# Four units of a recurrent projection begun early, their partial sums parked in SBUF

## The chip, the cores and the metric

One core of a Trainium2 chip. The metric is the device time of one execution in microseconds (us). Engines: PE is TensorE (matmul), PEld its weight loads, DVE VectorE, ACT ScalarE, POOL GpSimd, SP SyncE, which issues most transfers.

## What is computed

One inference step of a two-layer decoder trunk, width 1024, for a prompt of 512 tokens and 8 samples of 8 tokens. What matters here is the beginning of layer 0:

```python
sh1, sc1, g1, sh2, sc2, g2 = ada_mod(c, ada_w[l], ada_b[l], 6)     # silu(c) @ ada_w + ada_b, in six parts
h = modulate(rms_norm(x, norm_g[l, 0]), sh1, sc1)                   # h * (1 + scale) + shift
xr, yg = jnp.split(h @ w_in, 2, axis=-1)                            # w_in: 1024 x 2048
xr, new_buf = causal_dwconv(xr, conv_buf, conv_w, conv_b)           # width 4
o, h_last = rg_lru(xr, gate_w, gate_b, lam, h0)                     # gates (matmul, sigmoid), exp, sqrt, scan over time
out = (o * jax.nn.gelu(yg, approximate=True)) @ w_out
```

After it come a SwiGLU block, shared keys and values, a layer of sliding-window attention with a second SwiGLU block, and the final norm. Everything is float32.

## The kernel before

**Tiling.** Activations lie transposed: 128 channels on the partitions, tokens along the free dimension. The 1024 channels are 8 chunks; the tokens are two halves (h = 0 and 1) of 288 columns, 256 of the prompt and 32 of the samples. A weight unit (`Unit`, `unit_cols` L1059) is 8 x 128 rows by 128 columns, 512 KB, and makes one chunk of output for both halves. For accuracy each float32 operand is split into a rounded high part and the rest, the low part: `convert` (L1036) casts the weights' high part on ScalarE and subtracts on VectorE for the low one (tiles `wh` from `raw`), and `product` (L1075) runs three matmuls a chunk: high x high, high weights x low activations, low weights x high activations. A unit thus takes 24 matmuls of 128x288 a half, accumulated in one PSUM tile `mm`, of which there are six.

**The start.** Tokens are loaded, their squares summed (`x_half`, L1929: two tiles of each half's share on ScalarE or VectorE), turned by TensorE transposes into `x`, and `spread` (L871) makes the reciprocal root of the mean square with GpSimd's power and spreads it over the partitions (transposes, then ScalarE's copy to `acc`). The modulation of `c` is needed chunk pair by chunk pair: `ada_first_load` fetches four quarters of a pair's weights (2 MB a pair), `ada_first` (L769) multiplies them in matmuls of 32x128 into the PSUM tile `ada`, turns the result and puts it in `mods`. For each pair `modulated` (L881) makes the operand's high and low parts in tile `h`. While TensorE has nothing to do at the start it runs transposes of the identity (`keep_busy`), on which nothing waits.

**The recurrent block.** `RNN` (L56) gives the order: xN is unit N of the first half of `w_in`, whose sum `evac_xr` (L1115) copies out of PSUM on ScalarE to a tile `td` and convolves (one step on ScalarE, three on VectorE); gN are its gates (`gates`, L1141: three functions on ScalarE out of three table sets, six steps and a scan on VectorE); yN is unit N of the second half (`evac_yg`, L1205: gelu on ScalarE, product and split on VectorE). `decay_rates` (L694) makes the gates' constants out of `lam` with an exponential on ScalarE and 26 small steps on GpSimd.

**The order of the work.** All operations are recorded first (`Recorder`, L135); `schedule` (L231) then orders them over all engines by a list scheduler with costs in ns, program order, the tiles' free slots and biases that the code sets with `early(n)`. The result is a fixed program for each engine, which an engine runs in order. `record` (L434) writes every instruction, so that nearly all of them bear one line, L493, in the profile.

`LOADS` (L55) gives the order of the first transfers on SyncE's queue: pK are the modulation weights of pair K (digits after it name the quarters), xT the tokens, u the next weight unit: `units[0]` holds rows 0 to 511 of columns 0 to 255 (units 0 and 1), then unit 2, then rows 512 to 1023 of columns 0 to 255. The main part reads:

```python
    for c in range(0, KC, 2):
        ada_first(c, AF_[c // 2])
        for h in range(2):
            with early(E1):
                modulated(h, SC1, SH1, M1, slice(c, c + 2))
```

Of the kernel before, what the change touches and what calls it, by code (L numbers as in the profile page):

```python
# [19 lines left out]
P = 128  # L20
# [31 lines left out]
SPW = 60  # L52
WIN = 600

LOADS = "p0 u x2 x3 u p1 p201 u p223 p3"  # L55
RNN = "x0 x1 x2 x3 x4 x5 g0 g1 y0 y1 g2 g3 x6 y2 y3 g4 g5 x7 y4 y5 g6 g7 y7 y6"  # L56
ATT = "q0A q2A a0A q1A q0B a2A q1B q3A a0B q2B q4A a1A a1B a4A a3A q3B a2B q5A q4B a3B q6A a5A q5B q7A a6A a4B s0A a5B s1A s2A s3A q6B q7B a7A s0B s1B a6B fA a7B o0A s2B s3B o1A o2A fB"
LOOK = {"PE": 24, "DVE": 24, "ACT": 24, "POOL": 24, "SP": 24}
NRAW = 4
FILL = 250  # L60
DK = 200
AF_ = (1, 2, 2, 2)
NSL, NTA, NTB, NTD = 37, 7, 8, 4

# [455 lines left out]
def trunk_kernel(ctx, tc, a):  # L520
# [55 lines left out]
    @contextmanager  # L576
    def early(n):

        rec.bias -= n
        yield  # L580
        rec.bias += n
# [109 lines left out]
            s.done()  # L691


    def decay_rates():  # L694
        tw = sl()
        z, neg, p_, w_, w2, s_ = [tw.f[:, 8 * i : 8 * i + 8] for i in range(6)]
        pt = aux()
        T.transpose(pt[:, 0:8], lam, ident[0:8, 0:8])
        V.tensor_copy(lamT, pt[:, 0:8])
        lam_.done()  # L700
        G.tensor_scalar(neg, lamT, -1.0, None, ALU.mult)
        V.tensor_tensor(z, lamT, neg, ALU.max)
# [134 lines left out]
    def v48(t):  # L837
        return t.rearrange("p (b t) -> p b t", b=4)
# [18 lines left out]
    def stats(h):  # L857
# [10 lines left out]
        V.tensor_scalar(st[0:32, 2:3], pt[0:32, 2:3], 1.0 / D, EPS, ALU.mult, ALU.add)  # L868
        spread(h)

    def spread(h, r0=0):  # L871

        st, rs = tst[h][:, 0:3], tst[h][:, 3:6]
        G.tensor_tensor(rs, st, mhalf[:, 0:3], ALU.pow)
        o = aux()
        for t, ts in enumerate(TOK):
            r = slice(r0, r0 + 32) if t == 2 else ALL
            T.transpose(o[:, ts], rs[r, t : t + 1].to_broadcast([r.stop - r.start, P]), ident[r, r])
        S.copy(rstd[h][:], o[:, 0:HC])
# [231 lines left out]

    RN = [[None] * KC, [None] * KC]
    w_in = a["rnn_w_in"][0]

    def evac_xr(c):  # L1115
        def f(h, o):
            b_ = td()
            s1 = sl()
            RN[h][c] = s1
            b = b_.f  # L1120
            if h == 0:
                G.memset(b[:, 0:3], 0.0)
            else:
                G.tensor_copy(b[:, 0:3], cv5[:, 0, c, 0, :])
            S.copy(b[:, 3 : 3 + HP], o[:, 0:HP])
            sam = b[:, 259:303].rearrange("p (b t) -> p b t", t=11)
            S.copy(sam[:, :, 3:11], v48(o[:, HP:HC]))
            G.tensor_copy(sam[:, :, 0:3], scv[:, h, :, :, c])
            G.tensor_copy(cv5[:, h, c], b[:, 248:303].rearrange("p (b t) -> p b t", t=11)[:, :, 8:11])
            y = s1.f[:, 0:CW]  # L1130
            S.activation(y, b[:, 0:CW], AF.Identity, bias=cbT[:, c : c + 1], scale=cwT[:, 0, c : c + 1])
            for w in range(1, 4):
                V.scalar_tensor_tensor(y, b[:, w : w + CW], cwT[:, w, c : c + 1], y, ALU.mult, ALU.add)
            b_.done()
        return f
# [69 lines left out]
    def evac_yg(c):  # L1205
        def f(h, o):
            s0 = RN[h][c]
            t = ta()
            v = t.f[:, 0:HC]
            S.activation(v, o[:, 0:HC], AF.Gelu_apprx_tanh)  # L1210
            V.tensor_tensor(v[:, 0:HP], v[:, 0:HP], s0.f[:, 0:HP], ALU.mult)
            V.tensor_tensor(v48(v[:, HP:HC]), v48(v[:, HP:HC]),
                            s0.f[:, 259:303].rearrange("p (b t) -> p b t", t=11)[:, :, 0:8], ALU.mult)
            RN[h][c] = sl(F32R), sl(F32R)
            split(RN[h][c][0].r[:, 0:HC], RN[h][c][1].r[:, 0:HC], v)
            s0.done()
            t.done()
        return f
# [1 line left out]
    seq_ = RNN.split()  # L1220
    x01 = unit_pair(w_in, 0)
    x2 = unit_cols(w_in, 2 * P)
    units[1], units[2] = units[2], units[1]
    for i, w in enumerate(seq_):
        c = int(w[1:])
        if w[0] == "x":
            linear(x01[c] if c < 2 else x2 if c == 2 else unit_cols(w_in, c * P), hops, evac_xr(c))
        elif w[0] == "y":
            linear(unit_cols(w_in, D + c * P), hops, evac_yg(c))
        else:  # L1230
            first, last = ug[0] not in units, not any(v[0] == "g" for v in seq_[i + 1 :])
            if first:
                units.extend(ug)
            jobs.append(Job(0.75, gates(c), ug if first else (), ug if last else ()))
# [713 lines left out]


    keep_busy(aux(), 60)  # L1950
    with early(-DK):
        decay_rates()
    def load_one():
        load_more(nload[0] - nconv[0] + 1)

    kinds_ = (whs, whs, regs, whs)
    waits = {1: 0, 2: 150, 3: 200}
    n_ = 0
    for w in LOADS.split():
        if w[0] == "p":  # L1960
# [12 lines left out]
    for c in range(0, KC, 2):  # L1973
        ada_first(c, AF_[c // 2])
        for h in range(2):
            with early(E1):
                modulated(h, SC1, SH1, M1, slice(c, c + 2))
            if c == 0 and h == 0:
                with early(100):
                    x_half(1)  # L1980
                rec.idle_end()
    vectors_rest()

    setup = [False]

# [127 lines left out]
```

## Time and profile before

| | |
|---|---|
| median of 3 runs | 1250.93 us (1249.55 to 1251.86) |
| the profiled execution | 1252.16 us, its span in the trace 1249.4 us |
| instructions | 25384, of them 9599 matmuls |
| busy, of the span | PE 1234.5 us, PEld 1172.9, DVE 892.0, ACT 652.4, POOL 461.5 |
| moved by DMA | 165.39 MB, mean 132 GB/s |
| table loads on ACT | 21, of 1283 ns |

How to read it: a row of a timeline has start, duration, engine, line, operation, output<-inputs, shapes and a count of merged instructions; the bracket behind it is the idle time ahead and what ended it. Buffer numbers are left out, so that `wh<-raw` is every conversion of weights. A row of groups has count, busy time, mean duration of one in ns, idle time ahead. Matmuls overlap, so the duration of one (some 290 ns) is not its price in a row of them. The granted clock (PEclk) is 1.00 at full speed.

### The profile page before, as it was taken

The numbers are of one execution on the slowest core, as the hardware profiler recorded it, in microseconds if no ns is written. First come the engines' busy times: TensorE is split into PE (matmuls) and PEld (weight loads), VectorE is DVE, ScalarE is ACT, GpSimd is POOL, SyncE is SP. The second block draws the span as 40 slices with busy tenths as digits, with TensorE's granted clock in tenths as the row PEclk, the third lists the DMA queues.
The fourth block names the chain that finished last, engine by engine and source line by source line (L and its number), as shares of the span: only waits on it lengthen the run. The fifth ranks groups of instructions, "written<-read, shape, count | busy, mean of one in ns | idle before, by whom it ended". The sixth has DMA issues, their size and how long they took to land.

```text
span 1249.4 us, 25384 instructions
## 1 busy us (share of the span) xinstructions
PE 1234.5 (99%) x9599; PEld 1172.9 (94%) x9599; DVE 892.0 (71%) x2122; ACT 652.4 (52%) x1465; POOL 461.5 (37%) x635
## 2 busy tenths in 40 slices
PE   8999999999999999999999999999999999999997
PEld 6889899999999999999999988999999999999997
DVE  5887875896675676477579888558767667747766
ACT  4688853853343354145357679448425435515533
POOL 6353430153451453345125445100436246335500
PEclk9999999999999999999999999999999999999999
DMA  9975554426455545445423321422332323323222
GB/s 314 281 243 192 178 161 152 140 73 215 153 188 188 186 148 166 157 160 178 118 68 78 83 60 35 119 84 98 94 110 68 107 81 102 102 83 88 84 87 76
DMA packets 221868, 165.39 MB, mean 132 GB/s; under 512 B 23741, under 2 KB 207033, under 8 KB 221714
## 3 DMA queue, kind: packets, MB, share of 16 engines
q1 hardware_dynamic: 221266, 163.45, 42.8%
q8 instruction: 75, 1.23, 0.4%
q14 instruction: 47, 0.39, 0.1%
q0 software_dynamic: 480, 0.32, 0.1%
HBM read 160.85 MB, written 4.87 MB: 133 GB/s over the span
## 4 chain that ended last, share of the span: by engine, by line
PE 91%; DVE 3%; ACT 2%; POOL 2%; DMA 1%; issue 1%; DVEq 0%; ACTq 0%; POOLq 0%; SPq 0%
PE mm L493 86%; PE ada L493 5%; ACT sl L493 1%; DVE sl L493 1%; DVE wh L493 1%; POOL sl L493 1%; DVE ta L493 1%; ACT ta L493 1%; DMA raw<-in_ffn_w_in_dram 0%; DMA raw<-in_ffn_w_out_dram 0%; ACT wh L493 0%; POOL raw L493 0%; POOL ta L493 0%; DVE x L493 0%; ACT L493 0%
## 5 line engine op out<-in xcount | busy, mean ns | idle before, releaser
L493 PE MATMUL mm<-h,wh 128*128 128x288 f32 x4080 | 583.8, 297 | 1.8 <-DVE h L493 1.7
L493 PEld LDWEIGHTS mm<-h,wh 128*128 128x128 f32 x4080 | 553.7, 188 | 11.7 <-issue 6.6
L493 PE MATMUL mm<-sl,wh 128*128 128x288 f32 x3237 | 464.8, 296 | 0.4 <-ACT sl L493 0.3
L493 PEld LDWEIGHTS mm<-sl,wh 128*128 128x128 f32 x3237 | 439.8, 188 | 7.5 <-issue 5.9
L493 ACT CAST wh<-raw 128x512 fp32r<-128x512 f32 (+3 forms) x393 | 270.6, 708 | 294.9 <-PE mm L493 177.7
L493 DVE TENSOR_TENSOR wh<-raw,wh 128x512 fp32r<-128x512 f32 (+3 forms) x395 | 359.9, 931 | 58.4 <-ACT wh L493 53.5
L493 POOL TENSOR_TENSOR raw<-raw 128x512 f32<-128x512 f32 x78 | 114.8, 1472 | 175.8 <-DVE wh L493 158.3
L493 DVE SCALAR_TENSOR_TENSOR x<-mm,mods,x 128x256 f32<-128x256 f32 x160 | 77.2, 482 | 121.7 <-PE mm L493 120.9
L493 POOL TENSOR_TENSOR x<-x,ta 128x32 f32<-128x32 f32 x120 | 42.3, 352 | 242.4 <-DVE ta L493 242.3
L493 POOL TENSOR_TENSOR raw<-raw,raw 128x512 f32<-128x512 f32 x78 | 116.4, 1492 | 4.5
L493 PE MATMUL mm<-tb,wh 128*128 128x288 f32 (+1 forms) x500 | 92.0, 298 | 0.5 <-DVE td L493 0.5
L493 POOL TENSOR_TENSOR td<-td,td 128x288 f32<-128x288 f32 x39 | 32.6, 837 | 133.6 <-ACT td L493 120.4
L493 PEld LDWEIGHTS mm<-tb,wh 128*128 128x128 f32 x500 | 74.4, 188 | 3.1 <-DVE td L493 0.8
L493 PE MATMUL mm<-ta,wh 128*128 128x288 f32 (+1 forms) x259 | 57.4, 298 | 1.3 <-ACT ta L493 1.3
L493 ACT ACTIVATE ta<-x 128x288 f32<-128x288 f32 (+1 forms) x56 | 24.6, 443 | 64.5 <-POOL x L493 41.8
L493 DVE TENSOR_TENSOR td<-mm,td 128x288 f32<-128x288 f32 x78 | 34.4, 452 | 23.8 <-PE mm L493 23.3
L493 PE MATMUL ada<-reg,cz 128*32 128x512 f32 (+1 forms) x408 | 47.2, 547 | 0.0
L493 PEld LDWEIGHTS mm<-ta,wh 128*128 128x128 f32 x259 | 42.4, 188 | 3.7 <-ACT ta L493 2.8
L493 ACT ACTIVATE td<-td 128x288 f32<-128x288 f32 x39 | 17.3, 443 | 45.4 <-DVE td L493 45.3
L493 ACT COPY td<-mm 128x256 f32<-128x256 f32 (+1 forms) x103 | 33.9, 355 | 11.6 <-PE mm L493 9.8
L493 DVE TENSOR_TENSOR sl<-td,sl 128x288 fp32r<-128x288 f32 x49 | 33.4, 682 | 6.5 <-ACT sl L493 6.5
L493 ACT COPY ta<-mm 128x288 f32<-128x288 f32 (+1 forms) x51 | 19.1, 378 | 33.0 <-PE mm L493 31.9
(210 smaller groups left out, 1243.7 us busy)
## 6 DMA issues: line engine op xcount, KB each, us to landing
raw<-in_ffn_w_in_dram SPq DMA_DIRECT2D x88, 512.0 KB
reg<-in_ada_w_dram SPq DMA_DIRECT2D x72, 512.0 KB
raw<-in_ffn_w_out_dram SPq DMA_DIRECT2D x32, 384.0 KB
raw<-in_ffn_w_out_dram SPq DMA_DIRECT2D x32, 320.0 KB
raw<-in_rnn_w_in_dram SPq DMA_DIRECT2D x16, 512.0 KB
reg<-in_kv_ada_w_dram SPq DMA_DIRECT2D x14, 512.0 KB
wh<-in_ada_w_dram SPq DMA_DIRECT2D x24, 256.0 KB
raw<-in_rnn_w_out_dram SPq DMA_DIRECT2D x8, 512.0 KB
```

The costliest lines, as they stand in the source:

```text
L493: self.rec.add(eng, lambda: getattr(obj, name)(*map(real, args), **{k: real(v) for k, v in kw.items()}), cost, outs, ins, func, lat, port, ...
```

## The change

It has four parts.

1. A new unit `quad`: rows 0 to 255 (chunks 0 and 1) of the columns of units 3 to 6, 512 KB, loaded in the second place. As soon as a half's chunks 0 and 1 are modulated, `quad_parts` multiplies them with it, 24 matmuls a half, and ScalarE copies the four sums to tiles `sl`. Units 3 to 6 then hold six chunks (384 KB), and their sum is added to the parked one by VectorE on its way out of PSUM, where ScalarE copied before.
2. In the first norm the power on GpSimd is replaced by a square root on ScalarE and a reciprocal on VectorE. Later norms are as before.
3. `decay_rates` is recorded behind the second pair; only the turning of `lam` stays at the head.
4. `LOADS`, the conversions' biases and `RNN` are changed (x6, g3, y4 and y5 stand elsewhere); the gelu's result lies in `td`, not `ta`.

```diff
-LOADS = "p0 u x2 x3 u p1 p201 u p223 p3"
-RNN = "x0 x1 x2 x3 x4 x5 g0 g1 y0 y1 g2 g3 x6 y2 y3 g4 g5 x7 y4 y5 g6 g7 y7 y6"
+LOADS = "p0 u x2 x3 u p1 p201 p223 u u p3"
+QUAD = (3, 4, 5, 6)
+QK = 2
+RNN = "x0 x1 x2 x3 x4 x5 g0 g1 y0 y1 g2 x6 g3 y2 y3 g4 y4 g5 x7 y5 g6 g7 y7 y6"
...
     def spread(h, r0=0):
         st, rs = tst[h][:, 0:3], tst[h][:, 3:6]
-        G.tensor_tensor(rs, st, mhalf[:, 0:3], ALU.pow)
+        if not first_norm[0]:
+            G.tensor_tensor(rs, st, mhalf[:, 0:3], ALU.pow)
+        else:
+            S.activation(st, st, AF.Sqrt)
+            V.reciprocal(rs, st)
...
+    def quad_parts(h):
+        v = hops(h)
+        for j, c in enumerate(QUAD):
+            o = ps()[:, 0:HC]
+            for k in range(QK):
+                xh, xl = v[k]
+                hi, lo = [w.r[:, (k * len(QUAD) + j) * P :][:, 0:P] for w in (quad.hi, quad.lo)]
+                T.matmul(o, hi, xh, start=k == 0, stop=False)
+                T.matmul(o, hi, xl, start=False, stop=False)
+                T.matmul(o, lo, xh, start=False, stop=k == QK - 1)
+            PART[h, c] = sl()
+            S.copy(PART[h, c].f[:, 0:HC], o)
+        drop(quad)
...
-            S.copy(b[:, 3 : 3 + HP], o[:, 0:HP])
...
-            S.copy(sam[:, :, 3:11], v48(o[:, HP:HC]))
+            if c in QUAD:
+                q = PART.pop((h, c))
+                V.tensor_tensor(b[:, 3 : 3 + HP], o[:, 0:HP], q.f[:, 0:HP], ALU.add)
+                V.tensor_tensor(sam[:, :, 3:11], v48(o[:, HP:HC]), v48(q.f[:, HP:HC]), ALU.add)
+                q.done()
+            else:
+                S.copy(b[:, 3 : 3 + HP], o[:, 0:HP])
+                S.copy(sam[:, :, 3:11], v48(o[:, HP:HC]))
...
-    units[1], units[2] = units[2], units[1]
+    units[1:3] = [quad, units[2], units[1]]
...
+            if c in QUAD:
+                linear(unit_cols(w_in, c * P, QK, KC - QK), lambda h: hops(h)[QK:], evac_xr(c))
...
-    with early(-DK):
-        decay_rates()
+    lambdas()
...
-    waits = {1: 0, 2: 150, 3: 200}
+    waits = {1: 0, 2: 100, 3: 150, 4: 200}
...
+            if c + 2 == QK:
+                quad_parts(h)
...
+        if c == DKC:
+            decay_rates()
     vectors_rest()
+    first_norm[0] = False
```

What this does to the engines' programs, in three places. First TensorE, ahead of the second modulation pair (`ada`). Before (`h_391` is half 0's operand, `wh_373` and `wh_394` the high and low parts of the first unit, `wh_441` and `wh_452` those of unit 2; the transposes of `few` spread half 1's norm):

```order
38 L493 MATMUL mm_411<-h_391,wh_373 128x288
39 L493 MATMUL mm_411<-h_391,wh_394 128x288
40 L493 MATMUL mm_459<-ident,few 128x128 x2
41 L493 MATMUL mm_459<-ident,few 128x32
42 L493 MATMUL mm_411<-h_391,wh_373 128x288
43 L493 MATMUL mm_465<-h_391,wh_441 128x288 x2
44 L493 MATMUL mm_465<-h_391,wh_452 128x288
45 L493 MATMUL mm_465<-h_391,wh_441 128x288
46 L493 MATMUL mm_409<-h_391,wh_373 128x288
47 L493 MATMUL mm_409<-h_391,wh_394 128x288
48 L493 MATMUL ada_480<-wh_243,cz 32x128 x8
```

and now (`h_375` is half 0's operand, `wh_426` and `wh_442` are the high and low parts of the new unit, `mm_444`, `mm_448`, `mm_451` and `mm_491` its four sums):

```order
43 L497 MATMUL mm_444<-h_375,wh_426 128x288 x2
44 L497 MATMUL mm_448<-h_375,wh_426 128x288 x2
45 L497 MATMUL mm_451<-h_375,wh_426 128x288 x2
46 L497 MATMUL mm_444<-h_375,wh_442 128x288
47 L497 MATMUL mm_444<-h_375,wh_426 128x288 x2
48 L497 MATMUL mm_444<-h_375,wh_442 128x288
49 L497 MATMUL mm_448<-h_375,wh_442 128x288
50 L497 MATMUL mm_448<-h_375,wh_426 128x288 x2
51 L497 MATMUL mm_448<-h_375,wh_442 128x288
52 L497 MATMUL mm_476<-ident,few 128x128 x2
53 L497 MATMUL mm_476<-ident,few 128x32
54 L497 MATMUL mm_451<-h_375,wh_442 128x288
```

The new unit's products stand where those of units 0 to 2 were, and the first of them with a low part of the weights is row 46. Ten more follow row 53 ahead of the modulation block, which comes with all 64 matmuls in one piece; before, eight products stood in its middle. In all 36 products stand ahead of it, not 14.

Second VectorE over the same time. Before (`raw_423` is a square sum, `wh_452` the low part of unit 2's weights, `h_391` rows the low parts of half 0's operand):

```order
31 L493 ISA raw_423,few<-reg_125 128x1024
32 L493 ISA few 128x1
33 L493 COPY x_65<-mm_418 128x4x128
34 L493 TENSOR_SCALAR few<-few 128x2
35 L493 TENSOR_TENSOR h_391<-tb_381,h_391 128x2x32
36 L493 TENSOR_TENSOR h_391<-tb_384,h_391 128x256
37 L493 TENSOR_SCALAR tb_449<-ta_338,mods 128x256
38 L493 TENSOR_TENSOR wh_452<-raw_235,wh_441 128x1024
39 L493 TENSOR_TENSOR h_391<-tb_449,h_391 128x256
```

and now:

```order
31 L497 TENSOR_TENSOR h_375<-tb_367,h_375 128x2x32
32 L497 TENSOR_TENSOR h_375<-tb_370,h_375 128x256
33 L497 TENSOR_TENSOR h_375<-tb_373,h_375 128x256
34 L497 ISA raw_413,few<-reg_225 128x1024
35 L497 ISA few 128x1
36 L497 COPY x_65<-mm_400 128x4x128
37 L497 TENSOR_SCALAR few<-few 128x2
38 L497 TENSOR_TENSOR ta_439<-x_64,acc_69 128x64
39 L497 TENSOR_TENSOR wh_442<-raw_235,wh_426 128x1024
40 L497 RECIPROCAL few<-few 128x3
```

The operand's low parts now come ahead of the square sum, and half 1's mean square (row 37, then 40) behind it; the reciprocal stands behind the low part of the new unit.

Third VectorE at the third pair's modulation (`ada_722` and `mods`; `wh_720` and `wh_744` are the low parts of unit 2 and of the second part of units 0 and 1). Now:

```order
70 L497 TENSOR_TENSOR wh_720<-raw_424,wh_700 128x1024
71 L497 TENSOR_TENSOR h_508<-tb_704,h_508 128x2x32
72 L497 TENSOR_TENSOR ta_737<-x_65,acc_70 128x256
73 L497 TENSOR_TENSOR wh_744<-raw_432,wh_726 128x1024
74 L497 TENSOR_SCALAR tb_755<-ta_737,mods 128x256
75 L497 SCALAR_TENSOR_TENSOR mods<-ada_722,abT,vecT 128x9
76 L497 TENSOR_TENSOR h_508<-tb_755,h_508 128x256
77 L497 SCALAR_TENSOR_TENSOR mods<-ada_722,abT,vecT 128x9
```

Two conversions of weights stand shortly ahead of it; before it was one, that of the second part of units 0 and 1.

More of the change, by code (lines that the diff above doesn't have):

```diff
@@ L53 @@
 WIN = 600
-LOADS = "p0 u x2 x3 u p1 p201 u p223 p3"
-RNN = "x0 x1 x2 x3 x4 x5 g0 g1 y0 y1 g2 g3 x6 y2 y3 g4 g5 x7 y4 y5 g6 g7 y7 y6"
+LOADS = "p0 u x2 x3 u p1 p201 p223 u u p3"
+QUAD = (3, 4, 5, 6)
+QK = 2
+YT = lambda td, ta, sl: td
+RNN = "x0 x1 x2 x3 x4 x5 g0 g1 y0 y1 g2 x6 g3 y2 y3 g4 y4 g5 x7 y5 g6 g7 y7 y6"
 ATT = "q0A q2A a0A q1A q0B a2A q1B q3A a0B q2B q4A a1A a1B a4A a3A q3B a2B q5A q4B a3B q6A a5A q5B q7A a6A a4B s0A a5B s1A s2A s3A q6B q7B a7A s0B s1B a6B fA a7B o0A s2B s3B o1A o2A fB"
@@ L60 @@
 FILL = 250
-DK = 200
+DKC = 2
+XB = 100
 AF_ = (1, 2, 2, 2)
@@ L691, in vectors_rest, with lambdas @@
             s.done()
-    def decay_rates():
-        tw = sl()
-        z, neg, p_, w_, w2, s_ = [tw.f[:, 8 * i : 8 * i + 8] for i in range(6)]
+    def lambdas():
         pt = aux()
@@ L700, in decay_rates @@
         lam_.done()
+    def decay_rates():
+        tw = sl()
+        z, neg, p_, w_, w2, s_ = [tw.f[:, 8 * i : 8 * i + 8] for i in range(6)]
         G.tensor_scalar(neg, lamT, -1.0, None, ALU.mult)
@@ L869, in stats @@
         spread(h)
+    first_norm = [True]
     def spread(h, r0=0):
         st, rs = tst[h][:, 0:3], tst[h][:, 3:6]
-        G.tensor_tensor(rs, st, mhalf[:, 0:3], ALU.pow)
+        if not first_norm[0]:
[3 more added lines that the diff above has]
+            V.reciprocal(rs, st)
         o = aux()
@@ L1113, in trunk_kernel @@
     w_in = a["rnn_w_in"][0]
+    PART = {}
+    def quad_parts(h):
[11 more added lines that the diff above has]
+        drop(quad)
     def evac_xr(c):
@@ L1207, in f @@
             s0 = RN[h][c]
-            t = ta()
+            t = YT(td, ta, sl)()
             v = t.f[:, 0:HC]
@@ L1222, in trunk_kernel @@
     x2 = unit_cols(w_in, 2 * P)
-    units[1], units[2] = units[2], units[1]
+    q0 = QUAD[0] * P
+    quad = Unit(KC, [(ALL, slice(0, QK), slice(0, len(QUAD) * P), w_in[0 : QK * P, q0 : q0 + len(QUAD) * P].rearrange("(k p) n -> p k n", p=P))])
+    quad.n = len(QUAD) * P
+    units[1:3] = [quad, units[2], units[1]]
     for i, w in enumerate(seq_):
@@ L1226, in trunk_kernel @@
         if w[0] == "x":
-            linear(x01[c] if c < 2 else x2 if c == 2 else unit_cols(w_in, c * P), hops, evac_xr(c))
+            if c in QUAD:
+                linear(unit_cols(w_in, c * P, QK, KC - QK), lambda h: hops(h)[QK:], evac_xr(c))
+            else:
+                linear(x01[c] if c < 2 else x2 if c == 2 else unit_cols(w_in, c * P), hops, evac_xr(c))
         elif w[0] == "y":
@@ L1977, in trunk_kernel @@
                 modulated(h, SC1, SH1, M1, slice(c, c + 2))
+            if c + 2 == QK:
+                quad_parts(h)
             if c == 0 and h == 0:
-                with early(100):
+                with early(XB):
                     x_half(1)
                 rec.idle_end()
+        if c == DKC:
+            decay_rates()
     vectors_rest()
+    first_norm[0] = False
     setup = [False]
```

## The prediction

> **What bounds the kernel now.** I began with the page's chain of work that ended last:
>
> ```profile
> PE 91%; DVE 3%; ACT 2%; POOL 2%; DMA 1%; issue 1%; DVEq 0%; ACTq 0%; POOLq 0%; SPq 0%
> ```
>
> The kernel is a queue of matmuls on TensorE. A change pays by what it takes from that queue, or by filling time in which the queue is empty, and such time lies at the start. The table of stretches of 2 us (columns: stretch, busy us of PE, PEld, DVE, ACT, POOL with instructions, granted clock, DMA share, GB/s) shows where:
>
> ```profile
> 22.00:24.00 2.00, 0.87 (x5) 0.69 (x5) 2.00 (x6) 1.20 (x2) 1.59 (x5) 1.00 1.11 350
> 24.00:26.00 2.00, 0.06 (x1) 0.00 (x0) 1.61 (x5) 0.00 (x0) 1.92 (x4) 1.00 1.09 347
> 26.00:28.00 2.00, 1.99 (x10) 1.51 (x10) 0.92 (x2) 0.40 (x1) 1.27 (x4) 0.79 1.10 350
> 28.00:30.00 2.00, 2.00 (x34) 1.51 (x33) 1.94 (x8) 1.44 (x3) 1.68 (x6) 0.50 1.14 356
> 30.00:32.00 2.00, 2.00 (x28) 1.83 (x32) 0.56 (x2) 0.00 (x0) 0.00 (x0) 0.85 1.06 343
> ```
>
> From 22 to 26 us TensorE issues six matmuls, and after that rest its clock falls, to 0.50 at 28 to 30 us. Then TensorE's own timeline:
>
> ```profile
> 19.90 0.51 PE L493 MATMUL mm<-h,wh 128*128 128x288 f32 x2
> ...
> 23.13 0.93 PE L493 MATMUL mm<-h,wh 128*128 128x288 f32 x5 [1.40 <-DVE h L493]
> 26.01 0.60 PE L493 MATMUL mm<-ident,few 128*128 128x128 f32 x3 [1.95 <-POOL few L493]
> 26.54 1.54 PE L493 MATMUL mm<-h,wh 128*128 128x288 f32 x7
> ...
> 34.27 1.08 PE L493 MATMUL ada<-reg,cz 128*32 128x128 f32 x32
> 35.28 0.54 PE L493 MATMUL mm<-h,wh 128*128 128x288 f32 x2
> 36.08 3.31 PE L493 MATMUL mm<-h,wh 128*128 128x288 f32 x23 [0.27 <-DVE h L493]
> ...
> 46.89 0.79 PE L493 MATMUL mm<-h,wh 128*128 128x288 f32 x4
> 47.52 0.27 PE L493 MATMUL ada<-ident,ta 128*128 128x128 f32 x1
> 47.55 12.45 PE L493 MATMUL mm<-h,wh 128*128 128x288 f32 x91
> ```
>
> The last row gives the price of a product matmul where nothing is short: 12.45 / 91 = 0.137 us. Thirty-two modulation matmuls take 1.01 us (34.27 to 35.28). My mark is the transpose at 47.52, which turns the last modulation pair. From 19.90 to it pass 27.6 us, with 92 product matmuls (2 in the first row, 4 in the last, 86 between: 12.6 us), six blocks of 32 (6.1) and some 2 us of transposes (three take 0.53 at 26.01). So **6.9 us are lost**: 3.6 in the three waits in brackets, 2 x (0.21 + 0.50 + 0.15) = 1.7 to the slow clock, the rest to feeding like the two matmuls from 35.28 to 36.08.
>
> **The change, part by part.**
>
> *Early products.* Four sums over two chunks in three matmuls, for two halves: 48 x 0.137 = 6.6 us leave the stage behind the mark. That is the ceiling. The order of after has 125 product matmuls ahead of the same transpose, not 92: 33 x 0.137 = 4.5 us more. Without waits the mark would fall at 19.90 + 17.1 + 6.1 + 2 = 45.1 us. What the new order waits for needs VectorE's rows,
>
> ```profile
> 20.71 1.21 DVE L493 CUSTOM_DVE_ANT_0 raw<-reg 128x1024 f32<-128x1024 f32 x1
> 21.85 0.08 DVE L493 DVE_READ_ACCUMULATOR2_ANT few<- 128x1 f32 x1
> 21.85 0.68 DVE L493 COPY x<-mm 128x512 f32<-128x512 f32 x1
> 22.45 0.16 DVE L493 TENSOR_SCALAR few<-few 128x2 f32<-128x2 f32 x1
> 22.53 0.55 DVE L493 TENSOR_TENSOR h<-tb,h 128x64 fp32r<-128x64 f32 x2
> 23.00 0.40 DVE L493 TENSOR_SCALAR tb<-ta,mods 128x256 f32<-128x256 f32 x1
> 23.32 1.22 DVE L493 TENSOR_TENSOR wh<-raw,wh 128x1024 fp32r<-128x1024 f32 x1
> ```
>
> and two of ScalarE:
>
> ```profile
> 22.19 1.04 ACT L493 CAST wh<-raw 128x1024 fp32r<-128x1024 f32 x1
> 26.64 0.40 ACT L493 COPY acc<-mm 128x288 f32<-128x288 f32 x1 [3.41 <-PE mm L493]
> ```
>
> Up to 18.9 us nothing changes. Then VectorE does a 0.41 step, the first weights' low half (1.22), a copy (0.68) and the low halves of the operand (0.9): ready at 22.2, where before the last of them came after 24.46. The square sum (1.21), copy (0.68), two small steps (0.4) and the low half of the early weights (1.22) follow: 25.7. ScalarE's high half is ready at 23.3 as now. TensorE does 12 matmuls from 22.2, six high products to about 24.2, and waits for 25.7. So: wait for the operand 0.5 (21.7 to 22.2), wait for the low half **1.5**. A third comes at the third pair: two low halves (2 x 1.22) now stand ahead of its modulation on VectorE, where one stood; against 32 matmuls and a block of 32 on TensorE as cover I find 0.6 left (bounds 0 and 2.4). Other gaps 0.3. The slow clock costs 0 (no rest as long as now) to 1.7 (as now); the rest of 1.5 us is nearer to the present 1.40 and 1.95 in length, but matmuls now stand on both sides of it, so I take 0.4. Sum 3.3, the mark at 48.4: 0.9 later with 4.5 more done. **Lead 3.6 us.**
>
> The Trainium skill ("TensorE: Matmul & The Clock Gate", What's actually happening) says that the clock halves only after an idle window of about 3.4 us and returns after a busy one. By that the slow clock would cost nothing and the lead be 4.0; the trace agrees only in part, since the clock fell with no wait longer than 1.95 us.
>
> *Loads.* The early weights take the slot of unit 2 in SyncE's queue, the third pair's last loads go ahead of two units, and the last pair stands behind 0.52 MB more: at 347 GB/s 1.5 us later. TensorE turns to its second half about 1 us later than now; cost 0 to 0.5, taken as 0.
>
> *First norm.* GpSimd's power goes (row below), a square root and a reciprocal of the same three columns come.
>
> ```profile
> 24.89 1.06 POOL L493 TENSOR_TENSOR few<-few,small 128x3 f32<-128x3 f32 x1
> ```
>
> In half 1 it started 2.3 us after its input (22.45 + 0.16), behind the decay rates on GpSimd. But the reciprocal now stands behind the 1.22 us low half on VectorE and ends at 25.9, where the power ended at 25.95: nothing gained. Its copy to `acc` comes behind eight more matmuls and its transposes, near 28.0 instead of 27.0. The modulation block and the ten products ahead of it (to 30.8) hide that by about 0.5 us; without that cover it costs up to 1.0. In half 0 the power was not waited for. The decay rates are wanted by the first gates, tens of us later: nothing.
>
> *Tables.* The order of after lists 23 table loads instead of 21. The rows of one:
>
> ```profile
> 12.13 1.28 ACT L493 ACT_TABLE_LOAD   x1
> 13.43 0.21 ACT L493 ACTIVATE sl<-sl 128x8 f32<-128x8 f32 x1
> ```
>
> The next instruction follows 1.30 us after its start. The new one near 25 us lies beside the wait for the low half; the other, late in the gates, can cost 0 to 1.3. The Trainium skill ("ScalarE: Activation LUTs", What ACT_TABLE_LOAD costs) speaks against this change: each switch of set is said to cost about 2.66 us with a drain, so functions should be batched by set. The trace does not show the drain.
>
> *Conversion of the sums.* ScalarE takes eight sums out early, 8 x 0.40 = 3.2 us, among products that don't wait for them. Behind the mark it loses 16 copies and VectorE gets 16 additions. Groups of 48 to 166 us, of ScalarE and of VectorE, and the page's row for an addition out of PSUM:
>
> ```profile
> L493 ACT COPY td<-mm 128x256 f32<-128x256 f32 (+1 forms) x32 | 7.5, 286 | 4.5 <-PE mm L493 4.4
> ```
>
> ```profile
> L493 DVE TENSOR_TENSOR wh<-raw,wh 128x1024 fp32r<-128x1024 f32 x17 | 21.4, 1267 | 2.4 <-ACT wh L493 2.4
> ```
>
> ```profile
> L493 DVE TENSOR_TENSOR td<-mm,td 128x288 f32<-128x288 f32 x78 | 34.4, 452 | 23.8 <-PE mm L493 23.3
> ```
>
> ScalarE: -16 x 0.286 = -4.6. VectorE: a pair of 256 and 32 columns costs at least 0.452 and at most 0.452 + 0.286; I take 0.6, so 8 x 0.6 = +4.8, less a quarter of four low halves (4 x 0.32 = 1.3): **+3.5 us**. Does VectorE have them?
>
> ```profile
> 60.00:70.00 10.00, 10.00 (x80) 8.38 (x83) 9.83 (x14) 4.92 (x14) 9.82 (x15) 1.00 0.75 243
> ...
> 90.00:100.00 10.00, 10.00 (x79) 9.56 (x72) 4.89 (x9) 9.22 (x17) 1.35 (x4) 1.00 0.83 267
> ...
> 130.00:140.00 10.00, 9.54 (x72) 7.71 (x71) 9.71 (x20) 6.14 (x14) 8.04 (x18) 1.00 0.45 140
> ```
>
> At 60 to 70 us not (9.83), at 90 to 100 yes (5.1 idle). But the lead wants this stage to end 3.6 us sooner, so little is spare, and at 130 to 140 TensorE is already fed late: 72 instructions, not 79. I take 0.7 us off the lead. **Sum: -3.6 + 0.7 = -2.9.** The profiled execution took 1252.16 us (span 1249.4), 1.2 above the median of the runs, 1250.93; the same work in the median run gives **1248.0**.
>
> **The rivals.**
>
> *The gates bound the stage (0.15).* In each of the three rows above one of ScalarE and VectorE is 92 to 98% busy. If their chain, and not TensorE, sets the end, TensorE waits its lead away. For: 130 to 140 us. Against: TensorE shows 10.00 in the two stretches ahead. Gain 0 to 1: 1250.4.
>
> *The early products starve (0.08).* The change doesn't do what it says: the wait at 24 us keeps the clock down as now and the third pair's modulation costs the full 2.4 instead of 0.6. 3.6 - 1.3 - 1.8, and 0.5 more of the half-1 chain: no lead. 1250.9.
>
> *Slower: the additions (0.17).* The sums now leave PSUM by VectorE, behind convolution steps, at 98% load (60 to 70 us); six PSUM tiles fill, TensorE stops there, and the lead is spent. It decides from the point where VectorE's idle time at 90 to 100 us can't be used because it belongs to waits for ScalarE. Then the stage ends by the whole +3.5 later: 1254.4.
>
> *The drain (0.04).* If two further switches cost twice the 1.28 us of the row and both lie on the chain, 2.6 of the 2.9 go: 1250.7. The skill's 2.66 us is this case.
>
> *More than forecast (0.11).* The fuller order also feeds 130 to 170 us better; 72 against 79 instructions in 10 us are 1.0 us, twice that in all, and no 0.7 lost: 1245.4.
>
> **How the numbers follow.** The forecast gets 0.45, spread from 1246.5 to 1249.2; a measurement of this kernel can tell about 0.2%, 2.5 us, from no change, so 0.36 of it is faster and 0.09 the same. Faster: 0.36 + 0.11 = 0.47. Same: 0.09 + 0.15 + 0.08 + 0.04 = 0.36. Slower: 0.17. The range goes from 1245.2, the case of more, to 1253.6, into the slower case, and leaves out some 0.15. The forecast's own range is 1246.5 to 1249.2.
>
> **What would show it.** Right: 36 product matmuls ahead of the second pair's block instead of 14, a wait near 24.3 us of about 1.5 with the early low half as releaser, a granted clock above 0.8 at 26 to 32, the transpose of the last pair near 48.4, and TensorE at 10.00 in most stretches to 130 us. Wrong: a clock of 0.5 again; the mark after 50; TensorE waiting for VectorE's additions at 55 to 70; fewer than 72 instructions in the stretches of 130 to 170 us.

## The result and the profile after

| | before | after |
|---|---|---|
| median of 9 executions each, us | 1250.93 | 1247.53 |
| lowest to highest, us | 1249.42 to 1252.07 | 1247.09 to 1248.43 |
| ratio of the times, 95% interval | | 0.9979 (0.9970 to 0.9988) |
| profiled execution, us (span) | 1252.16 (1249.4) | 1247.53 (1245.8) |

By the medians the change made the kernel 3.4 us faster, 0.27%. The ratio in the table is an estimate of its own from the executions and not the quotient of the two medians; its interval allows 1.5 to 3.8 us. The executions of after lie closer together. After is more than before a queue of matmuls; its chain of work that ended last:

```profile
PE 94%; DMA 2%; DVE 2%; POOL 1%; ACT 1%; SPq 0%; issue 0%; DVEq 0%; POOLq 0%; ACTq 0%
```

The same stretches of 2 us, in the same columns:

```profile
22.00:24.00 2.00, 2.00 (x15) 1.76 (x13) 2.00 (x6) 1.77 (x4) 0.00 (x0) 1.00 1.11 349
24.00:26.00 2.00, 1.61 (x11) 1.29 (x10) 1.54 (x7) 1.46 (x4) 0.76 (x4) 1.00 1.10 348
26.00:28.00 2.00, 2.00 (x24) 1.77 (x27) 1.26 (x6) 1.63 (x5) 1.49 (x7) 1.00 1.10 348
28.00:30.00 2.00, 2.00 (x67) 1.80 (x56) 1.72 (x6) 1.09 (x4) 1.66 (x5) 1.00 1.10 348
30.00:32.00 2.00, 2.00 (x18) 2.00 (x17) 0.00 (x0) 0.86 (x3) 1.41 (x7) 1.00 1.12 338
```

From 22 to 26 us TensorE now has 26 instructions, not 6, and the granted clock stays at 1.00. TensorE's own timeline (start, length, in brackets the wait ahead and its releaser):

```profile
19.83 0.51 PE L497 MATMUL mm<-h,wh 128*128 128x288 f32 x2
...
21.57 2.55 PE L497 MATMUL mm<-h,wh 128*128 128x288 f32 x16
24.50 1.33 PE L497 MATMUL mm<-h,wh 128*128 128x288 f32 x8 [0.39 <-DVE wh L497]
25.67 0.60 PE L497 MATMUL mm<-ident,few 128*128 128x128 f32 x3
26.20 1.59 PE L497 MATMUL mm<-h,wh 128*128 128x288 f32 x10
...
36.27 1.87 PE L497 MATMUL mm<-h,wh 128*128 128x288 f32 x12 [0.41 <-DVE h L497]
...
38.00 3.16 PE L497 MATMUL mm<-h,wh 128*128 128x288 f32 x22
41.09 1.08 PE L497 MATMUL ada<-wh,cz 128*32 128x128 f32 x32
42.10 3.57 PE L497 MATMUL mm<-h,wh 128*128 128x288 f32 x25
...
47.24 0.27 PE L497 MATMUL ada<-ident,ta 128*128 128x128 f32 x1
47.27 10.92 PE L497 MATMUL mm<-h,wh 128*128 128x288 f32 x79
```

The two waits of 1.40 and 1.95 us are gone; what stands in their place is 0.39. The mark, the transpose of the last modulation pair (forecast at 48.4), falls at 47.24, 0.28 earlier than before, with 33 products more done: a lead of 0.28 + 4.5 = **4.8 us**.

From there I follow it to the first matmul of the recurrent output, which is the first `mm<-sl` row. The traces of before and after have the same matmuls ahead of it (720 products, 90 of the 96 of the gates, the same modulation blocks). In before and after it is

```profile
158.01 2.28 PE L493 MATMUL mm<-sl,wh 128*128 128x288 f32 x16
```

```profile
154.91 2.28 PE L497 MATMUL mm<-sl,wh 128*128 128x288 f32 x16
```

so 3.1 of the 4.8 us are left: **1.7 were lost in the gate stage**. After's table of stretches of 10 us shows where:

```profile
60.00:70.00 10.00, 10.00 (x80) 9.78 (x80) 9.80 (x16) 5.67 (x12) 8.38 (x13) 1.00 0.90 286
...
90.00:100.00 10.00, 10.00 (x76) 8.25 (x76) 6.83 (x12) 7.79 (x13) 0.81 (x5) 1.00 0.51 175
...
110.00:120.00 10.00, 7.85 (x56) 7.62 (x57) 8.41 (x18) 7.69 (x17) 6.02 (x6) 1.00 0.16 42
...
130.00:140.00 10.00, 10.00 (x78) 8.22 (x74) 9.31 (x19) 6.85 (x16) 8.91 (x20) 1.00 0.82 263
```

TensorE is full at 60 to 70 us, where I feared for it, and at 130 to 140 it is fed better than before (78 instructions, 72). It loses 2.15 us at 110 to 120. Its two waits there, and GpSimd's and VectorE's rows over the second:

```profile
110.46 0.41 PE L497 MATMUL mm<-tb,wh 128*128 128x300 f32 x1 [0.69 <-POOL tb L497]
...
119.13 0.55 PE L497 MATMUL mm<-tb,wh 128*128 128x300 f32 x2 [1.69 <-POOL tb L497]
```

```profile
115.57 3.51 POOL L497 TENSOR_TENSOR tb<-sl,ta 128x300 fp32r<-128x300 f32 x1 [3.06 <-PE mm L497]
```

```profile
115.30 0.45 DVE L497 TENSOR_TENSOR sl<-td,sl 128x288 fp32r<-128x288 f32 x1
115.67 1.22 DVE L497 TENSOR_TENSOR wh<-raw,wh 128x1024 fp32r<-128x1024 f32 x1
116.80 0.47 DVE L497 SCALAR_TENSOR_TENSOR sl<-tb,sl 128x300 f32<-128x300 f32 x1
117.19 1.22 DVE L497 TENSOR_TENSOR wh<-raw,wh 128x1024 fp32r<-128x1024 f32 x1
```

GpSimd works out the low part of a gate's operand, and one such subtraction took 3.51 us: it begins while VectorE is busy with the first of these rows, lasts through the three that follow without a gap, and ends 0.7 us behind the last of them.

### The profile page after: what moved, and what is told of

The parts are those of the page before. It is cut to its first block, busy times and chain, and to the rows that moved or that the text cites. A ratio compares the mean times of both kernels' runs of the same rounds, so it can differ in the third digit from the quotient of the medians.

```text
span 1245.8 us, 25395 instructions
## 1 busy us (share of the span) xinstructions
PE 1232.7 (99%) x9603; PEld 1171.4 (94%) x9603; DVE 895.3 (72%) x2141; ACT 655.5 (53%) x1462; POOL 461.9 (37%) x633
## 4 chain that ended last, share of the span: by engine, by line
PE 94%; DMA 2%; DVE 2%; POOL 1%; ACT 1%; SPq 0%; issue 0%; DVEq 0%; POOLq 0%; ACTq 0%
PE mm L497 89%; PE ada L497 5%; DMA reg<-in_x_prompt_dram 1%; DVE wh L497 1%; DMA wh<-in_ada_w_dram 0%; DMA raw<-in_ffn_w_out_dram 0%; POOL tb L497 0%; SPq L497 0%; DVE ta L497 0%; DVE h L497 0%; POOL sl L497 0%; DMA wh<-in_cache_k_dram 0%; DVE tb L497 0%; ACT wh L497 0%; POOL ta L497 0%
## 5 line engine op out<-in xcount | busy, mean ns | idle before, releaser
L497 DVE TENSOR_TENSOR sl<-td,sl 128x288 fp32r<-128x288 f32 x65 | 41.5, 642 | 7.9 <-ACT sl L497 7.6
L497 ACT ACTIVATE ta<-ta,stat 128x256 f32<-128x256 f32 (+2 forms) x72 | 32.5, 473 | 11.0 <-DVE stat L497 10.7
```

The lines of the kernel that those rows point to most:

```text
L497: self.rec.add(eng, lambda: getattr(obj, name)(*map(real, args), **{k: real(v) for k, v in kw.items()}), cost, outs, ins, func, lat, port, ...
```

## The experiments

Two places in the program divide the time: the *head*, from TensorE's first product (19.83 in after) to the mark, and the *stage*, from the mark to the first `mm<-sl` row. All numbers are read from TensorE's timeline of the one profiled execution of each run; "lost" is the stage against before's 110.49, less 0.137 us for each product done earlier, and corrected by 0.8 us (e5, e9, e10: six gate matmuls fewer ahead of the end) and by 1.9 (e6: sixteen modulation matmuls of 512 columns more, which take 1.93 us in after).

| kernel | ratio to before (95%) | products ahead of the mark | head | stage | lost |
|---|---|---|---|---|---|
| before | | 92 | 27.62 | 110.49 | 0 |
| after | 0.9979 (0.9970 to 0.9988) | 125 | 27.41 | 107.67 | 1.7 |
| e1: no early products | 1.0057 (1.0044 to 1.0069) | 94 | 24.54 | 119.49 | 9.3 |
| e2: early products alone | 0.9979 (0.9970 to 0.9987) | 126 | 27.60 | 106.22 | 0.4 |
| e3: before, more fillers | 0.9999 (0.9989 to 1.0009) | 89 | 27.97 | 110.91 | 0.0 |
| e4: low part on VectorE | 0.9998 (0.9989 to 1.0006) | 125 | 28.14 | 109.04 | 3.1 |
| e5: root and decay rates alone | 1.0003 (0.9994 to 1.0011) | 94 | 26.74 | 112.65 | 3.2 |
| e6: as e1, old tile | 1.0051 (1.0038 to 1.0065) | 94 | 26.12 | 118.83 | 6.7 |
| e7: after, old order and tile | 0.9967 (0.9955 to 0.9980) | 125 | 27.23 | 106.51 | 0.5 |
| e8: after, no additions | 0.9993 (0.9984 to 1.0002) | 125 | 27.22 | 109.73 | 3.8 |
| e9: before, VectorE copies | 0.9991 (0.9981 to 1.0000) | 92 | 25.40 | 108.84 | -0.8 |
| e10: e5, VectorE copies | 0.9997 (0.9988 to 1.0006) | 94 | 26.65 | 111.33 | 1.9 |
| e11: after again | 0.9981 (0.9972 to 0.9989) | 125 | 27.95 | 107.65 | 1.7 |
| e12: e7 again | 0.9976 (0.9967 to 0.9984) | 125 | 27.43 | 106.49 | 0.5 |

The stage repeats within 0.02 us (after and e11, e7 and e12). The head does not, as the text below e9 shows. The planner (`schedule`) sorts the whole program anew at each edit, so a kernel's stage differs by more than the edit; single differences below 1 us there prove nothing.

My theory, once the profile after was read: the gain is the empty time at 20 to 26 us, filled by the early products, with the clock kept up by it; the rest of the change is worth nothing. The rivals: GpSimd, freed of the power and the decay rates, carries part; or the new order and tile do; or ScalarE's relief by the additions does.

**e1, the change without its early products.**

```
-QUAD = (3, 4, 5, 6)
+QUAD = ()
 (and the loads, and the place of the units, as in before)
```

> The kernel after, without its early products: no parked sums, the loads in the order of before; the square root in the first norm, the decay rates behind the second pair, the new order of the recurrent units and the tile of the gated units stay. The order has 94 product matmuls ahead of the transpose of the last modulation pair (before 92, after 125). Theory (the gain is the empty time at 20 to 36 us, filled by the early products): the mark is again near 47.5, the clock falls again at 26 to 32 us, and the time is that of before, 1250.9, within 1.0. Rival (part of the gain comes from GpSimd, freed of the power and of the decay rates, and from the new order of the units): 1248.2 to 1249.5.

1257.01 us: neither. The change's other parts alone make the kernel 6.5 us slower. The head was shorter by 3.1 us, though, with 2 products more in it and the clock at 1.00:

```profile
22.69 0.93 PE L497 MATMUL mm<-h,wh 128*128 128x288 f32 x5 [1.10 <-DVE h L497]
23.58 0.60 PE L497 MATMUL mm<-ident,few 128*128 128x128 f32 x3
...
44.27 0.27 PE L497 MATMUL ada<-ident,ta 128*128 128x128 f32 x1
```

The wait of 1.95 us for the norm on GpSimd is gone without any early product: my theory of the head was too narrow. All of that, and some 6 us more, is lost in the stage, the longest wait there being 1.95 us for ScalarE at 107 us, behind which the granted clock fell to 0.50 (108 to 110 us). e5 and e6 say what makes it.

**e2, the early products alone.**

```
-YT = lambda td, ta, sl: td          +YT = lambda td, ta, sl: ta
-RNN = "... g2 x6 g3 y2 ..."         +RNN = "... g2 g3 x6 y2 ..."   (the old order)
-        if not first_norm[0]:       +        if True:              (power on GpSimd)
 (and decay_rates() at the head, put back by 200 places as in before)
```

> The kernel before with the early products, their loads and their additions alone: the power on GpSimd in the first norm, the decay rates at the head, the old order of the recurrent units and the old tile of the gated units. 126 product matmuls stand ahead of the mark. Theory (the early products carry the gain, the rest is worth nothing): 1247.5, within 1.0, the mark at 47 to 48. Rival (the rest carries part): 1249 to 1250.5. In this run the second half's first norm waits for GpSimd behind the decay rates again, so a wait of the kind of 1.95 us for its transposes would show what the square root was worth; with 24 products at hand in front of it I expect less than 0.5.

1247.44, as the theory had it (the mark at 46.73, a little ahead of the forecast), and no wait for the norm: the early products cover it. Together with their loads and their additions on VectorE, which this run has too, they carry the change; e8 takes the additions away. The stage loses 0.4, against 1.7 in after.

**e3, a cover of nothing.**

```
-    keep_busy(aux(), 60)
+    keep_busy(aux(), 120)
```

> The kernel before, with more of the matmuls on nothing that keep TensorE busy while it waits (94 used, not 60; 89 product matmuls ahead of the mark, not 92). They do no work of the kernel; only the clock can gain. Theory (1.7 us of the 6.9 lost ahead of the mark were the slow clock): the granted clock stays near 1.00 at 24 to 32 us, the mark falls to 46 to 46.7, and the time to 1249.2 to 1250, less 0.4 for the three products that come later. Rival (the slow clock cost nothing, since the products were short of operands and not of clock): the mark at 47.5 and 1250.9 to 1251.5.

Undecided: the median, 1249.45 against 1250.51 on that chip, lies in the theory's range, but the ratio with its interval (0.9999, 0.9989 to 1.0009) shows no gain. The profiled execution, at 1251.49 us the longest of the twelve, shows one reason: the fillers closed the wait at 22 us, but not that for GpSimd's norm (again 1.95 us), ahead of which the planner had put none, and the clock fell behind that alone. Seven of the twelve executions had a mean granted clock of 0.998 or more and took 1247.80 to 1249.92 us, the five others took 1250.56 or more; whether the seven had no such wait, no profile shows. Stretches of 2 us of the profiled one:

```profile
22.00:24.00 2.00, 2.00 (x17) 1.90 (x17) 2.00 (x9) 1.53 (x2) 1.57 (x6) 1.00 1.10 348
24.00:26.00 2.00, 0.33 (x3) 0.09 (x1) 1.48 (x2) 0.00 (x0) 1.92 (x3) 1.00 1.11 349
26.00:28.00 2.00, 1.73 (x12) 1.23 (x16) 0.66 (x4) 0.46 (x2) 1.12 (x5) 0.85 1.11 350
28.00:30.00 2.00, 2.00 (x33) 1.52 (x30) 2.00 (x7) 1.38 (x3) 0.76 (x1) 0.50 1.09 350
```

**e4, GpSimd's subtractions given to VectorE.**

```
-            G.tensor_tensor(xl.r[:, 0:CW], xc, xh.f[:, 0:CW], ALU.subtract)
+            V.tensor_tensor(xl.r[:, 0:CW], xc, xh.f[:, 0:CW], ALU.subtract)
```

> The kernel after, with the low part of the gate operands (16 subtractions of 300 columns) on VectorE and not on GpSimd. Theory (about 1.2 us of the lead were lost to TensorE's two waits of 1.69 and 0.69 us for GpSimd's subtraction at 110 to 119 us, which took up to 3.5 us for want of the memory port that it shares with VectorE): these waits go, the subtractions take 0.3 to 0.5 us each, and the time is 1246.3, within 0.7. Rival 1 (VectorE has no room; 16 x 0.4 = 6.4 us more on it turn up as waits elsewhere in the stage): 1248 to 1251. Rival 2 (the waits at 110 to 119 us were given back later in any case): 1247.5.

1249.51: rival 1. The waits for `tb` went, and one longer wait of 2.42 us came at 139 us, for ScalarE, with a slow clock behind it (0.84 at 140 to 150 us): the stage loses 3.1 instead of 1.7. VectorE is 9.95 of 10 us busy at 130 to 140 us. GpSimd's late operand is where after loses its lead, but giving the work to VectorE does not keep it.

**e5, the root and the moved decay rates alone.** As e1, with the old order and the old tile.

> The kernel before with the square root in the first norm and the decay rates behind the second pair alone: no early products, the old loads, the old order of the recurrent units, the old tile of the gated units. 94 product matmuls stand ahead of the mark. Theory (the root and the moved decay rates, too, take away the empty time at 24 to 26 us, and a lead at the mark is kept when the order of the units and the tile are the old ones): the mark near 44.3, the clock at 1.00, the stage behind it without long waits, and 1247.4, within 1.0. Rival (a lead of 3.5 us at the mark cannot be kept, because ScalarE and GpSimd bound the recurrent stage without the early products): 1250 to 1252. Rival of the first theory (the gain is the early products' alone): 1250.9 with the mark at 47.5.

1250.50: the rival. In the profile there is no wait for the norm, but the mark came at 46.24, not at 44.3, since the operand was waited for (1.69 us) and the clock fell behind that, to 0.52 at 24 to 26 us. The lead at the mark (1.3 us and two products, 1.6 in all) is lost in the stage. Of the 3.2 us lost there, TensorE's wait for ScalarE at 111 us is one large piece; behind it the clock fell again, to 0.70 and 0.50 in the two stretches from 112 to 116 us, and that accounts for most of the rest (3.2 less this wait and one of 0.34 leaves 1.3, an estimate):

```profile
111.82 0.66 PE L497 MATMUL mm<-ident,ta 128*128 128x128 f32 x4 [1.53 <-ACT ta L497]
```

Against e1, which differs in order and tile, it is 6.5 us faster.

**e6, which of the two it is.** As e1, with `YT = lambda td, ta, sl: ta`.

> The kernel after without its early products, as in the run of 1257.0, but with the old tile of the gated units; the new order of the recurrent units stays. Theory (TensorE's waits of 1.95 and 1.34 us for ScalarE's gated units at 107 and 143 us come from the new tile, whose four buffers the convolutions hold too): those waits go, and the time is 1247.5 to 1249. Rival (the new order of the units made the loss): 1256 to 1258.

1257.01: the rival. The new order of the units makes the loss, not the tile; the waits only change their names (3.42 us for ScalarE's `ta` at 109). Without the early products the order costs 6.5 us in the medians (e1 and e6 against e5); beside them, order and tile together cost 1.2 in the stage (e7, e12).

**e7, after with the old order and tile.**

> The kernel after with the old order of the recurrent units and the old tile of the gated units: early products, square root and moved decay rates stay. 125 product matmuls ahead of the mark, as in after. Theory (root and early products fill the same empty time, so the two do not add up; the new order is worth nothing beside the early products): the mark at 47.2, 1247.5 within 1.0. Rival 1 (the two add up): the mark below 45 or 1244 to 1245. Rival 2 (the new order and tile are what makes room for the additions): 1249 or more.

1246.83: the theory. With early products in place the root adds nothing that the intervals can tell (e2: 0.9979; e7 and its repetition e12: 0.9967 and 0.9976). Both measures are aimed at the same empty time: the wait of 1.95 us for the norm is missing from all profiles with the root (e1, e5, e6, e10) and from all with the early products; of the three with neither, before and e3 have it and e9 has not. How much the root shortens the head by itself is not shown: its heads, 24.54 to 26.74 us, lie on both sides of e9's 25.40 below, which has no root.

**e8, after without the additions.**

```
-                V.tensor_tensor(b[:, 3 : 3 + HP], o[:, 0:HP], q.f[:, 0:HP], ALU.add)
-                V.tensor_tensor(sam[:, :, 3:11], v48(o[:, HP:HC]), v48(q.f[:, HP:HC]), ALU.add)
+                S.copy(b[:, 3 : 3 + HP], o[:, 0:HP])
+                S.copy(sam[:, :, 3:11], v48(o[:, HP:HC]))
```

> The kernel after, without adding the parked sums: ScalarE copies the four sums out of PSUM as it does for the other units, so the first two chunks of four recurrent units are left out of the result, while all matmuls stay. It prices the 16 additions on VectorE. Theory (TensorE never waited for the additions; what was lost in the gate stage was GpSimd's): 1247.5, within 0.7. Rival (the 3.5 us more on VectorE cost the lead that is gone at 110 to 119 us): 1246 to 1246.5. Rival on the other side (16 copies more on ScalarE, which bounds the stage as much): 1249 or more.

1249.79: the rival on the other side. The additions do not cost, they pay: with the sums on ScalarE the stage loses 3.8 instead of 1.7, and the shortest execution (1249.26 us) is longer than the longest of after's twenty (1248.97). The waits for GpSimd are not in this order; instead TensorE waits 0.91 and 1.22 us for ScalarE (115 and 139 us) and 0.77 for VectorE (104). So the early products without the additions keep 1.2 of their 5.0 us of lead, and the ratio is not clear of 1: here the gain needed both, the early products to make the lead and the relief of ScalarE to keep it. (This holds for the new order of the units; the old one was not tried without the additions.) The groups of 48 to 155 us, of after on ScalarE and VectorE and of e8 on ScalarE:

```profile
L497 ACT COPY td<-mm 128x256 f32<-128x256 f32 (+1 forms) x16 | 3.6, 282 | 0.7 <-PE mm L497 0.7
```

```profile
L497 DVE TENSOR_TENSOR td<-mm,sl 128x256 f32<-128x256 f32 (+1 forms) x16 | 4.3, 297 | 1.2 <-PE mm L497 1.2
```

```profile
L497 ACT COPY td<-mm 128x256 f32<-128x256 f32 (+1 forms) x32 | 7.5, 287 | 4.8 <-PE mm L497 4.8
```

**e9 and e10, the relief of ScalarE by itself.** In before (e9) and in e5 (e10) the same four units' sums are copied by VectorE:

```
-            S.copy(b[:, 3 : 3 + HP], o[:, 0:HP])
+            (V.tensor_copy if 3 <= c < 7 else S.copy)(b[:, 3 : 3 + HP], o[:, 0:HP])
 (and the second copy likewise)
```

> The kernel before, with one edit: the sums of four recurrent units (the four that the change adds up on VectorE) are copied out of PSUM by VectorE, not by ScalarE: 16 instructions change engine, nothing else. Theory (the gate stage is bound by ScalarE as soon as TensorE has a lead; before has none at the mark, so there is little to win): 0 to 1.3 us, the waits of 0.46, 0.42 and 0.40 for ScalarE at 137, 144 and 162 us: 1249.5 to 1250.7. Rival (the relief of ScalarE is the gain of the change): 1247.5. Rival on the other side (VectorE is the tighter engine at 60 to 70 us): 1252 or more.

> The kernel with the root norm and the moved decay rates alone, which stood at 1250.5 and lost its lead of 1.55 us at the mark behind a wait of 1.53 for ScalarE at 111 us; now with the same four sums copied by VectorE. Theory (the lead is lost to ScalarE's queue and kept when ScalarE is relieved): 1248.5 to 1249.2, no wait over 1 us for ScalarE at 100 to 125 us. Rival (the lead is lost to the gates' chain as a whole, whichever engine copies): 1250.5, within 0.7.

e9: 1249.36, as the theory had it (1249.24 without one execution of 4217 us, which the ratio leaves out); e10: 1250.18, as the rival, though the wait at 112 us shrank from 1.53 to 0.53 and the clock stayed at 1.00 behind it. In the stage the copies gain 0.8 and 1.3 us, e8 had 2.1 with the other sign: ScalarE's relief is worth about 1 to 2 us there in the profiles, too little to stand out clearly in the medians of e9 and e10.

e9 showed something else. Its order up to the mark is before's, row for row on TensorE, VectorE, ScalarE and GpSimd; yet its profiled execution had no wait for the norm, and the mark at 45.75 instead of 47.52. Its times run from 1245.94 to 1250.90. GpSimd's rows, of before and then of e9 (8-column steps of the decay rates, and the norm's power):

```profile
19.12 1.66 POOL L493 TENSOR_TENSOR ta<-x,acc 128x256 f32<-128x256 f32 x1
20.75 1.24 POOL L493 TENSOR_TENSOR sl<-sl 128x8 f32<-128x8 f32 x1
22.07 0.23 POOL L493 TENSOR_SCALAR sl<-sl 128x8 f32<-128x8 f32 x1
...
23.55 1.08 POOL L493 TENSOR_SCALAR sl<-sl 128x8 f32<-128x8 f32 x1
```

```profile
18.56 0.72 POOL L493 TENSOR_TENSOR ta<-x,acc 128x256 f32<-128x256 f32 x1
...
19.53 1.08 POOL L493 TENSOR_SCALAR sl<-sl 128x8 f32<-128x8 f32 x1
...
21.30 1.01 POOL L493 TENSOR_TENSOR sl<-sl 128x8 f32<-128x8 f32 x1
...
23.02 1.13 POOL L493 TENSOR_TENSOR few<-few,small 128x3 f32<-128x3 f32 x1
```

In these two traces a step of 0.2 us takes over 1 us when it meets one of VectorE's long instructions (in before the square sum of 1.21 us at 20.71 and the low half of 1.22 at 23.32, whose rows the prediction shows). In e9 the chain met them otherwise, and the power began at 23.02, not at 24.89. The largest part of these 1.87 us is the first row, the step of 256 columns: 1.66 us in before, 0.72 in e9. In before it met VectorE's low half of the first weights, in e9 that low half came behind it, since ScalarE had waited for the load of these weights. VectorE in before, then ScalarE and VectorE in e9:

```profile
18.98 1.22 DVE L493 TENSOR_TENSOR wh<-raw,wh 128x1024 fp32r<-128x1024 f32 x1
```

```profile
18.21 1.04 ACT L493 CAST wh<-raw 128x1024 fp32r<-128x1024 f32 x1 [1.21 <-DMA raw<-in_rnn_w_in_dram]
```

```profile
19.29 1.23 DVE L493 TENSOR_TENSOR wh<-raw,wh 128x1024 fp32r<-128x1024 f32 x1 [0.79 <-ACT wh L493]
```

So before does not have one head but several. In the runs here it took 1246.93 to 1252.45 us, after 1247.09 to 1248.97 in both its sets: the best executions are alike, and what the change takes away is the bad ones. The mean granted clock of an execution goes with its time: of the 85 executions of before beside the experiments, the 13 with a clock of 0.998 took 1246.93 to 1249.07 us, the 72 others, with 0.995 to 0.997, had a median of 1250.80; all twenty of after have 0.998 or more. That the bad ones are those with the wait for the norm is what the profiles of before and e9 suggest, not more.

**e11 and e12, after and e7 side by side.**

> The kernel after, unchanged, beside the next run on the same chip: 1247.5, within 0.5, and its profile once more. If GpSimd's subtractions of up to 3.5 us at 109 to 119 us belong to the order and not to one execution, the waits of 0.69 and 1.69 us stand there again.

> The kernel after with the old order of the recurrent units and the old tile of the gated units, unchanged from its first run (1246.83). Theory (the new order and the new tile are worth nothing): within 0.3 of after on the same chip. Rival (they cost a part of what the early products bring): 0.5 to 1.0 below after, as the first runs stood (0.9967 against 0.9979).

1247.92 and 1247.59. The waits of 0.69 and 1.69 us stand in e11 at 111.2 and 119.9 us: they belong to the order. e7's order loses 1.2 us less in the stage, twice; in the medians it is 0.3 us ahead of after side by side, between the theory and the rival, and 0.7 in the first runs, less than their intervals can tell. It is the fastest kernel here, by a margin that isn't settled. GpSimd's subtractions over the whole program, of after and of e7 (count, us, mean ns):

```profile
L497 POOL TENSOR_TENSOR tb<-sl,ta 128x300 fp32r<-128x300 f32 x16 | 20.4, 1282 | 12.5 <-ACT ta L497 9.2 <-PE mm L497 3.1 <-issue 0.3
```

```profile
L497 POOL TENSOR_TENSOR tb<-sl,ta 128x300 fp32r<-128x300 f32 x16 | 15.6, 982 | 13.8 <-ACT ta L497 13.5 <-PE mm L497 0.2
```

## Why the prediction was right, and where it wasn't

- **The mechanism** held: the early products fill TensorE's empty time, and the lead they make is carried to the end, less a part (e2, and after's timeline). The additions on VectorE, which the prediction counted as a cost, are part of that: without them little of the lead is left (e8). 1247.53 stands within 0.5 us of 1248.0. 36 products stand ahead of the second pair's block (2, 16, 8 and 10 in the rows above), the early low half is the releaser of the wait at 24.5, and the clock is 1.00.
- **The lead** was mis-sized: 3.6 forecast, 4.8 in the profile. The wait for the low half of the early weights was 0.39 (0.55 in e11), not 1.5; the third pair's 0.6 did not come (22 products and a block cover it from 38.00 to 42.10, and the 25 products behind them start without a wait); of the slow clock's 0.4 nothing came. The wait for the operand (0.5 at 22) did not come either. A wait of 0.41 at 36 us stood in the 0.3 of others. I had VectorE's low half end at 25.7; it ended at 24.45 (25.25 in e11), since the square sum began at 21.28 and not at 22.2, and steps in a row overlap by some 0.1 us each. The other end of this wait was off as well: at 0.137 us each, the 18 products that I counted from 22.2 end at 24.7, not 24.2, so by its own figures the wait should have been 1.0.
- **The slow clock's price** was 1.7 in the sum of what was lost. Four kernels with the same order to the mark (e1, e5, e6, e10) give it: from the end of the wait at 23 us to the mark e1 took 21.58 us with the clock at 1.00, the others 22.67, 22.72 and 22.69 with 0.50 to 0.52 for a time. So 1.1.
- **First norm: nothing gained** held for the time beside the early products (e2 against e7). The reading behind it did not: the reciprocal ended at 24.54, not at 25.9, and the half-1 copy at 26.71, not at 28.0; nothing waited for them. Without the early products, none of the four profiles with the root and the moved decay rates has the wait for the norm (e1, e5, e6, e10), while two of the three without them have it (before and e3, not e9); that they work on the same empty time as the early products was not said.
- **Conversion of the sums** is the step that failed. I took 0.7 us off the lead for 3.5 us more on VectorE. The additions cost what I said (4.3 us for 16, forecast 4.8), but ScalarE's 16 copies fewer were worth more: without them the stage is 2.1 us longer (e8). The rival that the additions make it slower had the wrong engine.
- **What was lost instead** was 1.7 us, 2.4 in two waits for GpSimd's operand (e11 repeats them), which no step of the prediction named. It comes with the new order and tile: e7, without them, loses 0.5. The rival "the gates bound the stage" is half true: the gates' chain ate 1.7 of this lead's 4.8, but all of e5's and 3.8 of 5.0 of e8's.
- **The median.** The sum was made against one execution of before, at 1252.16, and carried over to the median as the same number of us. Before's head varies by some 2 us between executions (27.62 in its profile, 25.40 in e9's, same order), so the lead, head against head, is 4.7 or 2.5 us according to which one is compared; after's own head was 0.5 longer in e11. Against the profile of before, that -2.9 met -3.4 rests on a lead forecast too small by 1.2 and a loss forecast too small by 1.0: two errors that nearly cancel, so that the closeness of the number is in part luck.
- **Loads and tables** at 0 to 1.3 us: nothing in after's waits points to either; neither was tried alone.

What stays open: why the new order of units, without early products, costs 6.5 us (e1, e6). The waits are seen, at 107 and 143 us and at 109; what in the planner makes them was not tried.

## What to carry to other kernels

Two measures aimed at the same empty time need not add up (here the second was worth nothing that could be measured); price each with the other in place. Work moved to another engine has two ends: read what the relieved engine does with the time, here worth more than the burdened one lost. And where executions of one kernel differ by more than the expected gain, look for what the longer ones wait for: work ready to fill that wait is worth most there.

## What the runs showed of the hardware

- A GpSimd subtraction of 300 columns took 0.82 us (e6, at its shortest) and 3.51 beside VectorE's two conversions of 1.22 us and a step of 0.47 (after): 0.82 + 2.91 = 3.7, close to a full wait for these three. The Trainium skill ("SBUF — State Buffer", Who interferes with whom) says that a VectorE instruction with two inputs in SBUF contends with a GpSimd instruction that reads SBUF, and that VectorE and GpSimd share a port pair under an exclusive lock. The traces agree as to who is slowed. That the subtraction waited for all three, and not only for the step under way when it began, is what the sum of the durations suggests.
- The clock fell after rests of TensorE of 1.26 us (e9), 1.49 (e6) and 1.69 (e5) at the start, but not after 1.10 there (e1). In the gate stage it fell after 1.53 (e5 at 112 us) and 1.95 (e1 at 107 us), but not after 1.51 (e2 at 104 us) or 1.69 (after at 119 us). So the length of one rest does not decide it. The Trainium skill ("TensorE: Matmul & The Clock Gate", What's actually happening) speaks of a free-running window of about 3.4 us; none of these rests is as long, so by the rule as I used it the clock should have stayed up.
